# A decoder block on one core: biases in the constant pack, x in four 4 KB-row tiles, half of the transposes behind p's first step

## Chip, cores and metric

The kernel runs on one core of a Trainium2 chip. The metric is device time in microseconds (us), the median of three runs. Before the change it is 675.62 us (675.38 to 676.07).

## What is computed

One residual block on 512 tokens of width 1024. The change touches its front alone: the modulation by `c`, the first normalisation, and the start of the input projection.

```python
c_act = jax.nn.silu(c)
mod = c_act @ ada_w[l] + ada_b[l]
shift1, scale1, gate1, shift2, scale2, gate2 = [m[:, None, :] for m in jnp.split(mod, 6, axis=-1)]
h = rms_norm(x, norm1_g[l]) * (1 + scale1) + shift1
z = h @ w_in[l]
q, k, v, p, g_attn, g_pool = jnp.split(z, split_at, axis=-1)
```

Attention, pooling mixer, gates, output projection and the feed-forward part follow and are the same before and after.

## The kernel before

All is float32. A large product is made of three matmuls: each operand is split into a rounded part (`hi`, on ScalarE, called ACT) and the rest (`lo`, on VectorE, called DVE), and hi.hi, hi.lo and lo.hi are summed in one PSUM bank. There are eight banks of 128 x 512 floats. TensorE is called PE, GpSimd POOL, SyncE SP.

The block's input `h` is wanted transposed: eight tiles `h[k]` of 128 features x 512 tokens. The front makes them so:

- `crow` is silu(c). Two matmuls of a row of ones with it put c on all 128 partitions; ACT copies them to `cbc` (L234).
- x comes as eight tiles of 128 tokens x 512 features, in rows of 2 KB (L164). `rms_rows` sums the squares of a token's two halves, the first on ACT, the second on DVE (L174, L176), adds them on DVE (L180) and takes the power -1/2 on POOL (L182). `scale_x` multiplies each half by it: the first on ACT (L220), the second on DVE (L222), of the last token tile both on ACT (L224).
- PE transposes the scaled x in 32 pieces of 128 x 128 into the eight banks `xT` (L242), token tile by token tile, all before the first matmul of the projection.
- `ada_sum` (L191) makes one modulation value for each of 128 features: DVE multiplies a tile of 128 rows of `ada` by `cbc` and sums along the row. A row holds 1026 floats: 1024 weights, the bias, and a 1 for the two scales (0 elsewhere), and `cbc` ends in two ones, so that the sum is already bias and 1 + scale. There are 48 such tiles, 16 of them (shift and scale for k = 0 to 7) in the front.
- `make_x(k)` copies `xT[k]` out of PSUM with the norm's gain (ACT L248; k = 7 on DVE, L250). `make_h(k)` applies scale and shift on ACT (L280), rounds to `h[k]` hi (L282), and `lo_h` gives the rest on DVE (L287). For k = 0, `gs` (L293) holds gain times scale and `make_h` reads `xT[0]` itself.

The projection's first two products, p (four banks, 128 features each) and q (four banks, 128 tokens each), run k by k: twelve matmuls of p (L135, L138), then twelve of q. Their weights come as tiles p0, q0 (k = 0, 1), p1, q1 and so on, and are split into hi (ACT L109, p0 on DVE L107) and lo (L119: on DVE, q1's on POOL).

PE, ACT and DVE run in the order in which the code is written, each its own; this order is set by hand. The loads are issued by SP in the order of `queue`, and a buffer of the five `wraw` must be free (`pump`): a new load follows a sum or a split. The weights' hi and lo tiles have four buffers each.

Of the kernel before, what the change touches and what calls it, by code (L numbers as in the profile page):

```python
# [51 lines left out]
def block_kernel(tc, x, cvec, ada, wtok, wch, pool_w, wbr, wout, wup, wdn, pack, table, out):  # L52
    nc = tc.nc
# [3 lines left out]
    with ctx:  # L57
        ctx.enter_context(tc.manual_schedule(engines=ENG))
        ep = lambda *a, **k: ctx.enter_context(tc.tile_pool(*a, **k))
        cpool = ep(name="const", bufs=1)  # L60
# [85 lines left out]
        cbc = cpool.tile([P, AW], F32, name="cbc")  # L146
        nc.vector.memset(cbc[:, D:], 1.0)
# [11 lines left out]
        xt = []
        for t in range(TT):  # L160
            row = []
            for f in range(2):
                xi = slot(f"x_{t}_{f}")
                nc.sync.dma_start(xi, x[t * P : (t + 1) * P, f * 512 : (f + 1) * 512])  # L164
                row.append(xi)
            xt.append(row)

        def rms_rows(tiles, name):

            ss = mini.tile([P, 2], F32, tag="ss", name=f"ss_{name}")  # L170
            for f in range(2):
                junk = slot(f"junk_{name}_{f}")
                if f == 0:
                    nc.scalar.activation(junk, tiles[f], AF.Square, scale=1.0 / math.sqrt(D), accum_out=ss[:, f : f + 1])  # L174
# [42 lines left out]
        rss, cbs = [], []  # L217

        def scale_x(t):
            nc.scalar.activation(xt[t][0], xt[t][0], AF.Copy, scale=rss[t])  # L220
            if t < TT - 1:
                nc.vector.tensor_scalar(xt[t][1], xt[t][1], rss[t], None, op0=ALU.mult)  # L222
            else:
                nc.scalar.activation(xt[t][1], xt[t][1], AF.Copy, scale=rss[t])  # L224

        for t in range(TT):
            rs = rms_rows(xt[t], f"x{t}")
            if t < 2:
                cbs.append(bank(f"cb_{t}"))
                nc.tensor.matmul(cbs[t], ones, crow[:, t * 512 : t * 512 + 512], start=True, stop=True)  # L230
            if t:
                scale_x(t - 1)
                if t < 3:
                    nc.scalar.activation(cbc[:, (t - 1) * 512 : t * 512], cbs[t - 1], AF.Copy)  # L234
            rss.append(rs)
        scale_x(TT - 1)

        hh, hl, xs, araw = [], [], {}, {}
        xT = [bank(f"xT_{k}") for k in range(KT)]
        for t in range(TT):  # L240
            for k in range(KT):
                nc.tensor.transpose(  # L242
                    xT[k][:, tslice(t)], xt[t][k // 4][:, (k % 4) * P : (k % 4 + 1) * P], ident)

        def make_x(k):
            xs[k] = slot(f"xs_{k}")
            if k < KT - 1:
                nc.scalar.activation(xs[k], xT[k], AF.Copy, scale=col(C_N1 + k))  # L248
            else:
                nc.vector.tensor_scalar(xs[k], xT[k], col(C_N1 + k), None, op0=ALU.mult)  # L250
# [56 lines left out]
        qps = [bank(f"q_{t}") for t in range(TT)]
        pps = [bank(f"p_{g}") for g in range(TT)]
        for k in range(KT):
            i = k // 2  # L310
# [415 lines left out]
        for t in range(TT):  # L726
            for f in range(2):
                if (t, f) == (0, 0):
                    for t_ in range(2):
                        for f_ in range(2):  # L730
                            out_mm(t_, f_, 0, KT - 2)
                if (t, f) != (3, 0):
                    out_mm(t, f, KT - 2 if t < 2 else 0, KT)
                    out_post(t, f, ops[t, f])
                if late:
                    ada_col(4, late.pop(0))
                    if not late:
# [223 lines left out]
def _layout(a):  # L961
# [32 lines left out]
    arr["pack"] = c(np.concatenate(
        [cols(one("norm1_g")), cols(one("norm2_g")), qk("q_norm_g"), qk("k_norm_g"),
         cols(one("pool_scale")), inv, np.eye(P, dtype=np.float32), cw, cols(one("conv_b"))], axis=1))
# [28 lines left out]
```

## Time and profile before

| | |
|---|---|
| median of three runs | 675.62 us |
| the profiled execution, its time | 675.27 us |
| its span in the profile | 673.3 us |
| PE busy | 662.5 us (98% of the span) |
| DVE, ACT, POOL busy | 518.2, 333.5, 91.8 us |
| HBM read, written | 114.11, 15.75 MB |

The profile is one execution. Its span runs from the first instruction to the last; the time has 2 us more around it. An engine's busy time counts its instructions, not its waits. Names like L191 are lines of the kernel before.

### The profile page before, as it was taken

The page shows a single profiled execution, that of the slowest core. Times are in us where ns is not written, and L with a number is a line of the kernel's source. Part 1 is how long each engine was busy: PE and PEld are TensorE (multiplying, and loading weights), DVE is VectorE, ACT ScalarE, POOL GpSimd, SP SyncE. Part 2 cuts the span into 40 slices and gives each one's busy share as a digit, 9 for nine tenths or more (in the row PEclk, how much of TensorE's full clock was granted, in tenths as well). Part 3 has the DMA queues.
Part 4 walks back from the last instruction along what each step waited for, and adds up shares of the span by engine and source line. Part 5 has one row for each costly group of instructions (what it writes and reads, how often), then busy time and mean ns, then how long its engine had stood idle before and what let it go on. Part 6 is the DMA issues. An engine that isn't in the chain of part 4 may idle for free.

```text
span 673.3 us, 8771 instructions
## 1 busy us (share of the span) xinstructions
PE 662.5 (98%) x3106; PEld 551.4 (82%) x3106; DVE 518.2 (77%) x853; ACT 333.5 (50%) x536; POOL 91.8 (14%) x120
## 2 busy tenths in 40 slices
PE   6999999999999999999999999999999999999997
PEld 4778788888888788888998888888888888888885
DVE  5786876887877688876578878878787878878774
ACT  6545256765564656503653443425344344767431
POOL 2202150000000054603011111120110000001000
PEclk9999999999999999999999999999999999999999
DMA  8795231355543366693257675866835445667741
GB/s 314 274 329 210 93 127 64 109 168 169 176 146 110 94 220 208 193 350 140 80 213 263 212 250 191 307 222 225 298 132 187 165 149 170 213 222 265 250 180 59
DMA packets 41505, 130.43 MB, mean 194 GB/s; under 512 B 5251, under 2 KB 5420, under 8 KB 41462
## 3 DMA queue, kind: packets, MB, share of 16 engines
q1 hardware_dynamic: 35270, 109.82, 47.4%
q0 software_dynamic: 6192, 20.06, 9.0%
q8 instruction: 24, 0.39, 0.2%
q14 instruction: 19, 0.16, 0.1%
HBM read 114.11 MB, written 15.75 MB: 193 GB/s over the span
## 4 chain that ended last, share of the span: by engine, by line
PE 95%; ACT 2%; DVE 1%; issue 1%; DMA 1%; SPq 0%; POOL 0%; DVEq 0%
PE u L129 12%; PE u L128 12%; PE u L130 12%; PE gate_ps L129 4%; PE gate_ps L128 4%; PE gate_ps L130 4%; PE X L892 3%; PE X L890 3%; PE X L891 3%; PE o L128 2%; PE o L130 2%; PE o L129 2%; PE O L495 2%; PE Y L892 1%; PE Y L890 1%; PE Y L891 1%
## 5 line engine op out<-in xcount | busy, mean ns | idle before, releaser
L128 PE MATMUL u<-h2h,hi_up 128*128 128x512 f32 (+1 forms) x384 | 142.7, 372 | 0.0
L129 PE MATMUL u<-h2l,hi_up 128*128 128x512 f32 (+1 forms) x384 | 142.7, 372 | 0.0
L130 PE MATMUL u<-h2h,lo_up 128*128 128x512 f32 (+1 forms) x384 | 142.7, 372 | 0.0
L128 PEld LDWEIGHTS u<-h2h,hi_up 128*128 128x128 f32 x384 | 72.4, 188 | 12.6
L130 PEld LDWEIGHTS u<-h2h,lo_up 128*128 128x128 f32 x384 | 72.4, 188 | 12.5
L129 PEld LDWEIGHTS u<-h2l,hi_up 128*128 128x128 f32 x384 | 72.4, 188 | 12.4
L191 DVE CUSTOM_DVE_ANT_0 raw_ada<-raw_ada,cbc 128x1026 f32<-128x1026 f32 x48 | 60.9, 1293 | 2.9 <-DMA raw_ada<-in_ada 2.6
L760 ACT ACTIVATE uv<-u,pk 128x512 f32<-128x512 f32 x22 | 17.1, 780 | 85.8 <-PE u L130 85.8
L119 DVE TENSOR_TENSOR lo_up<-raw_up,hi_up 128x1024 fp32r<-128x1024 f32 x44 | 52.0, 1219 | 5.8 <-ACT hi_up L109 5.8
L130 PE MATMUL gate_ps<-h_h,lo_gate 128*128 128x512 f32 x128 | 50.0, 390 | 0.0
L129 PE MATMUL gate_ps<-h_l,hi_gate 128*128 128x512 f32 x128 | 49.9, 390 | 0.0
L128 PE MATMUL gate_ps<-h_h,hi_gate 128*128 128x512 f32 x128 | 49.9, 390 | 0.0
L109 ACT ACTIVATE hi_up<-raw_up 128x1024 fp32r<-128x1024 f32 x44 | 44.2, 1048 | 4.3 <-PE u L129 4.3
L813 POOL DMA_DIRECT2D tsum_t<-b x44 | 23.8, 540 | 145.1 <-DVE b L808 138.9
L761 DVE SCALAR_TENSOR_TENSOR uv<-u,pk,uv 128x511 f32<-128x511 f32 x22 | 16.5, 749 | 34.2 <-ACT uv L760 34.2
L119 DVE TENSOR_TENSOR lo_t<-raw_t,hi_t 128x1024 fp32r<-128x1024 f32 (+1 forms) x24 | 26.6, 1129 | 10.4 <-ACT hi_t L109 10.4
L760 ACT ACTIVATE ug<-u,pk 128x512 f32<-128x512 f32 x22 | 17.0, 775 | 32.2 <-PE u L130 32.2
L204 POOL TENSOR_TENSOR wo_l<-raw_wo,wo_h 128x512 fp32r<-128x512 f32 x16 | 25.6, 1619 | 53.6 <-ACT wo_h L203 53.6
L109 ACT ACTIVATE hi_t<-raw_t 128x1024 fp32r<-128x1024 f32 (+1 forms) x24 | 23.7, 987 | 17.9 <-PE Y L892 8.8
L130 PEld LDWEIGHTS gate_ps<-h_h,lo_gate 128*128 128x128 f32 x128 | 24.0, 188 | 5.1
L128 PEld LDWEIGHTS gate_ps<-h_h,hi_gate 128*128 128x128 f32 x128 | 24.0, 188 | 4.6
L129 PEld LDWEIGHTS gate_ps<-h_l,hi_gate 128*128 128x128 f32 x128 | 24.1, 188 | 4.5
(255 smaller groups left out, 1511.3 us busy)
## 6 DMA issues: line engine op xcount, KB each, us to landing
raw_ada<-in_ada SPq DMA_DIRECT2D x48, 513.0 KB, 5.0
raw_up<-in_wup SPq DMA_DIRECT2D x44, 512.0 KB, 4.9
b<-in_wdn SPq DMA_DIRECT2D x44, 256.0 KB, 5.6
tsum_t<-b POOLq DMA_DIRECT2D x44, 256.0 KB, 2.8
raw_t<-tsum_t SPq DMA_DIRECT2D x20, 512.0 KB, 4.5
raw_gate<-in_wch SPq DMA_DIRECT2D x16, 512.0 KB, 5.0
raw_b<-in_wdn SPq DMA_DIRECT2D x15, 512.0 KB, 3.4
raw_br<-in_wbr SPq DMA_DIRECT2D x8, 512.0 KB, 4.5
```

Of the source, the lines that this page charges most:

```text
L109: nc.scalar.activation(hi, raw, AF.Copy)
L119: (nc.gpsimd if nm in pool else nc.vector).tensor_sub(lo, raw, hi.bitcast(F32))
L128: nc.tensor.matmul(ps, sh, mh, start=start, stop=False)
L129: nc.tensor.matmul(ps, sh, ml, start=False, stop=False)
L130: nc.tensor.matmul(ps, sl, mh, start=False, stop=stop)
L191: nc.vector.tensor_tensor_reduce(out=raw, in0=raw, in1=cbc, op0=ALU.mult, op1=ALU.add, scale=1.0, scalar=0.0, accum_out=acol[:, i : i + 1])
L204: (eng or nc.vector).tensor_sub(lo[:, :w], src, hi[:, :w].bitcast(F32))
L760: nc.scalar.activation(t, ps, AF.Identity, scale=cw(2), bias=col(C_CB + i))
L813: nc.gpsimd.dma_start(tsum[n, i][:, u * 512 : u * 512 + 512], b[nm])
L890: nc.tensor.matmul(ps, sh, mh, start=start, stop=False, skip_group_check=True)
L891: nc.tensor.matmul(ps, sh, ml, start=False, stop=False, skip_group_check=True)
L892: nc.tensor.matmul(ps, sl, mh, start=False, stop=stop, skip_group_check=True)
```

## The change

Three things are changed.

1. The biases go to the constant pack (48 columns, `C_AB`), and a row of `ada` has 1024 floats. `ada_sum` starts its sum from the bias (`scalar=`). The 1 of 1 + scale is added by an instruction of its own on DVE for k = 1 to 7, and inside `gs` for k = 0.
2. x comes as four tiles of 128 x 1024, in rows of 4 KB. They lie in two buffers of the hi and two of the lo weights. Each token tile's second half is scaled on DVE, the last one's too.
3. Of the 32 transposes only those of k = 0 to 3 stand ahead of p's k = 0; the other 16 follow it, and q's k = 0 follows them. For k = 0, `h[0]` hi is made on ACT directly from the bank, and the unrounded value on DVE from the bank too. p's k = 0 takes its lo weights before its lo inputs. q1's lo part is made on DVE.

```diff
-                out=raw, in0=raw, in1=cbc, op0=ALU.mult, op1=ALU.add, scale=1.0, scalar=0.0,
+                out=raw, in0=raw, in1=cbc, op0=ALU.mult, op1=ALU.add, scale=1.0, scalar=col(C_AB + i),
...
+        def load_x(t):
+            xi = (whi_p if t < 2 else wlo_p).tile([P, 1024], F32, tag="hi" if t < 2 else "lo", name=f"x_{t}")
+            nc.sync.dma_start(xi, x[t * P : (t + 1) * P])
...
         def sum_h(k):
             for g in range(2):
-                ada_sum(g, k, araw[g, k])
-                held[0] -= 1
-                pump()
+                sum_one(g, k)
+                if g:
+                    nc.vector.tensor_scalar(acols(1, k), acols(1, k), 1.0, None, op0=ALU.add)
...
         def split(name, **kw):
-            ahead(name, 0, pool=("q1",), **kw)
+            ahead(name, 0, **kw)
...
+        scale_x(3, 0, False)
+        flip_x(3, 0)
+        sum_one(0, 0)
+        scale_x(3, 1, True)
+        sum_one(1, 0)
+        gs = mini.tile([P, 1], F32, tag="gs", name="gs")
+        nc.vector.tensor_scalar(gs, acols(1, 0), 1.0, col(C_N1), op0=ALU.add, op1=ALU.mult)
+        make_x(1)
+        his["p0"] = hi_of("p0", early["p0"], True)
...
+        nc.scalar.activation(hh[0], xT[0], AF.Identity, scale=gs, bias=acols(0, 0))
+        split("p0")
+        nc.vector.tensor_scalar(xs[0], xT[0], gs, acols(0, 0), op0=ALU.mult, op1=ALU.add)
         lo_h(0)
...
         sum_h(1)
         split("q0")
         make_h(1)
         lo_h(1)
         sum_h(2)
-        qps = [bank(f"q_{t}") for t in range(TT)]
         pps = [bank(f"p_{g}") for g in range(TT)]
...
+            if k == 0:
+                for k2 in range(4, KT):
+                    xT[k2] = bank(f"xT_{k2}")
+                for t in range(TT):
+                    flip_x(t, 4)
+                for k2 in range(4, KT):
+                    make_x(k2, k2 == 7)
+                qps = [bank(f"q_{t}") for t in range(TT)]
...
-    arr["ada"] = c(np.concatenate(
-        [one("ada_w").T, one("ada_b")[:, None], unit.reshape(6 * D, 1)], axis=1)).reshape(48, P, AW)
+    arr["ada"] = c(one("ada_w").T).reshape(48, P, D)
```

Two places show what the new order does. The first is PE's list around p's and q's k = 0. Before (repeats left out; the brackets name the engines whose signal is awaited), the last transpose, p and q stand in a row, and q's four banks `q_290` to `q_293` wait for ACT alone:

```order
L242 MATMUL xT_190<-pk,x_1_130 128x128
L135 MATMUL p_294<-h_h,hi_p_246 128x512 [waits DVE_49,PE_49,Activation_49]
L135 MATMUL p_297<-h_h,hi_p_246 128x512 [waits DVE_49]
L138 MATMUL p_297<-h_h,lo_p_248 128x512
L135 MATMUL q_290<-hi_q_261,h_h 128x512 [waits Activation_49]
L135 MATMUL q_292<-hi_q_261,h_h 128x512 [waits Activation_49]
L135 MATMUL q_293<-hi_q_261,h_h 128x512 [waits Activation_49]
```

Now p's k = 0 ends, 16 transposes go to the four banks of k = 4 to 7 (`xT_271` to `xT_274`), and q's first four matmuls write the same four banks one after the other:

```order
L138 MATMUL p_258<-h_l,hi_p_214 128x512
L267 MATMUL xT_271<-pk,x_116 128x128 [waits PE_49]
L267 MATMUL xT_274<-pk,x_116 128x128 [waits Activation_49]
L267 MATMUL xT_274<-pk,x_122 128x128
L135 MATMUL q_299<-hi_q_226,h_h 128x512 [waits Activation_49]
L135 MATMUL q_300<-hi_q_226,h_h 128x512 [waits Activation_49]
L135 MATMUL q_301<-hi_q_226,h_h 128x512 [waits Activation_49]
L135 MATMUL q_302<-hi_q_226,h_h 128x512 [waits DVE_49]
L138 MATMUL q_299<-hi_q_226,h_l 128x512
```

What moved: q's k = 0 stood behind p's k = 0 alone; it now stands behind 16 transposes too, and its fourth bank waits for a copy that DVE makes.

The second place is DVE's list from p0's lo part on. Before, the copy of `xT[7]` (`xs_267`) stands ahead of the sums for k = 1 (`raw_ada_231`, `raw_ada_234`) and k = 2 (`raw_ada_237`, `raw_ada_250`):

```order
L119 TENSOR_TENSOR lo_p_248<-raw_p_227,hi_p_246 128x1024 [waits DVE_49]
L287 TENSOR_TENSOR h_l<-xs_241,h_h 128x512 [waits Activation_49]
L250 TENSOR_SCALAR xs_267<-xT_190,pk 128x512 [waits PE_49]
L191 ISA raw_ada_231,acol<-raw_ada_231,cbc 128x1026 [waits DMAHW5_49]
L191 ISA raw_ada_234,acol<-raw_ada_234,cbc 128x1026 [waits DMAHW7_49]
L119 TENSOR_TENSOR lo_q_275<-raw_q_229,hi_q_261 128x1024 [waits DMAHW4_49,Activation_49]
L287 TENSOR_TENSOR h_l<-xs_253,h_h 128x512 [waits Activation_49]
L191 ISA raw_ada_237,acol<-raw_ada_237,cbc 128x1026 [waits DMAHW0_49]
L191 ISA raw_ada_250,acol<-raw_ada_250,cbc 128x1026 [waits DMAHW1_49,DVE_49]
```

Now it stands behind them (`xs_297`, last row), with the additions of 1 (L240) in between:

```order
L119 TENSOR_TENSOR lo_p_220<-raw_p_128,hi_p_214 128x1024 [waits DVE_49]
L306 TENSOR_SCALAR xs_216<-xT_134,gs,acol 128x512 [waits PE_49,Activation_49]
L263 TENSOR_TENSOR h_l<-xs_216,h_h 128x512 [waits DVE_49]
L190 ISA raw_ada_132,acol<-raw_ada_132,cbc,pk 128x1024 [waits DMAHW2_49]
L190 ISA raw_ada_204,acol<-raw_ada_204,cbc,pk 128x1024 [waits DMAHW3_49]
L240 TENSOR_SCALAR acol<-acol 128x1 [waits DVE_49]
L119 TENSOR_TENSOR lo_q_239<-raw_q_130,hi_q_226 128x1024 [waits DMAHW0_49,Activation_49]
L263 TENSOR_TENSOR h_l<-xs_212,h_h 128x512 [waits Activation_49]
L190 ISA raw_ada_208,acol<-raw_ada_208,cbc,pk 128x1024 [waits DMAHW4_49]
L190 ISA raw_ada_222,acol<-raw_ada_222,cbc,pk 128x1024 [waits DMAHW7_49,DMAHW5_49,DVE_49]
L250 TENSOR_SCALAR xs_297<-xT_274,pk 128x512 [waits PE_49]
```

What moved: the copy of the eighth bank went from before the four sums of k = 1 and 2 to behind them, and one copy of the first bank (`xs_216`) came to DVE.

## Rows read from the trace of the kernel before

**Rows 1.** The page: busy time by engine, share of the span, instructions.

```profile
PE 662.5 (98%) x3106; PEld 551.4 (82%) x3106; DVE 518.2 (77%) x853; ACT 333.5 (50%) x536; POOL 91.8 (14%) x120
```

**Rows 2.** Waits of PE, whole span: total us, times, longest.

```profile
PE p L135 <- ACT h_h L282: 1.4, 2, 0.9
```

**Rows 3.** Timeline of PE, front: start us, us, instruction.

```profile
10.17 5.09 PE L242 MATMUL xT<-pk,x 128*128 128x128 f32 x25 [0.43 <-ACT cbc L234]
15.80 1.94 PE L135 MATMUL p<-h_h,hi_p 128*128 128x512 f32 x4 [0.55 <-ACT h_h L282]
...
19.42 1.29 PE L135 MATMUL q<-hi_q,h_h 128*128 128x512 f32 x4
...
22.39 1.07 PE L135 MATMUL p<-h_h,hi_p 128*128 128x512 f32 x4
...
32.36 1.07 PE L138 MATMUL q<-lo_q,h_h 128*128 128x512 f32 x4
34.33 1.19 PE L135 MATMUL p<-h_h,hi_p 128*128 128x512 f32 x4 [0.90 <-ACT h_h L282]
...
56.67 1.07 PE L135 MATMUL p<-h_h,hi_p 128*128 128x512 f32 x4
```

**Rows 4.** Timeline of DVE, front.

```profile
9.68 0.48 DVE L222 TENSOR_SCALAR x<-x,rs_x 128x512 f32<-128x512 f32 x1
10.09 0.69 DVE L176 CUSTOM_DVE_ANT_0 junk_x<-x 128x512 f32<-128x512 f32 x1
...
11.38 1.23 DVE L191 CUSTOM_DVE_ANT_0 raw_ada<-raw_ada,cbc 128x1026 f32<-128x1026 f32 x1
...
13.91 0.16 DVE L293 TENSOR_TENSOR gs<-acol,pk 128x1 f32<-128x1 f32 x1
...
16.45 0.74 DVE L250 TENSOR_SCALAR xs<-xT,pk 128x512 f32<-128x512 f32 x1
17.11 1.22 DVE L191 CUSTOM_DVE_ANT_0 raw_ada<-raw_ada,cbc 128x1026 f32<-128x1026 f32 x1
...
19.40 1.22 DVE L119 TENSOR_TENSOR lo_q<-raw_q,hi_q 128x1024 fp32r<-128x1024 f32 x1
21.56 0.69 DVE L287 TENSOR_TENSOR h_l<-xs,h_h 128x512 fp32r<-128x512 f32 x1 [0.94 <-ACT h_h L282]
...
24.46 0.08 DVE L191 DVE_READ_ACCUMULATOR2_ANT acol<- 128x1 f32 x1
```

**Rows 5.** Timeline of ACT, the making of h for k = 1.

```profile
20.02 0.84 ACT L280 ACTIVATE xs<-xs,acol 128x512 f32<-128x512 f32 x1
```

**Rows 6.** DMA, us to landing: first x tile (issued at 1.14), first modulation tile (4.88).

```profile
x<-in_x SPq DMA_DIRECT2D x1, 256.0 KB, 2.6
...
raw_ada<-in_ada SPq DMA_DIRECT2D x1, 513.0 KB, 6.5
```

**Rows 7.** Front in three stretches: busy us of PE, PEld, DVE, ACT, POOL; PEclk, DMA share, GB/s.

```profile
4.50:5.50 1.00, 1.00 (x3) 0.48 (x2) 0.00 (x0) 0.01 (x1) 0.00 (x0) 1.00 1.06 404
5.75:8.25 2.50, 1.67 (x4) 0.27 (x2) 1.92 (x7) 1.77 (x4) 0.94 (x2) 1.00 0.89 272
10.10:15.20 5.10, 5.03 (x25) 4.85 (x25) 4.90 (x12) 3.43 (x8) 1.20 (x2) 1.00 1.02 414
```

**Rows 8.** Timeline of DVE, two sums from 28 us on.

```profile
28.19 3.42 DVE L191 CUSTOM_DVE_ANT_0 raw_ada<-raw_ada,cbc 128x1026 f32<-128x1026 f32 x1
...
31.54 1.22 DVE L191 CUSTOM_DVE_ANT_0 raw_ada<-raw_ada,cbc 128x1026 f32<-128x1026 f32 x1
```

**Rows 9.** Timeline of POOL, q1's lo part and the four fills.

```profile
28.04 2.49 POOL L119 TENSOR_TENSOR lo_q<-raw_q,hi_q 128x1024 fp32r<-128x1024 f32 x1 [16.19 <-ACT hi_q L109]
30.59 2.03 POOL L400 MEMSET kz<- 64x512 f32 x4
```

**Rows 10.** The front transposes, 10.1 to 14 us: count, ns min/median/max, first and last start.

```profile
L242 PE MATMUL xT<-pk,x x18: 421/421/478, 10.2 to 13.9; 128*128 128x128 f32 x18
```

**Rows 11.** Later transposes of the same size, same columns.

```profile
L688 PE MATMUL hT<-pk,xn x32: 270/272/274, 313.5 to 328.1; 128*128 128x128 f32 x32
```

More of the change, by code (lines that the diff above doesn't have):

```diff
@@ L45 @@
 C_ID = C_INV + 64
-C_EARLY = C_ID + P
+C_AB = C_ID + P
+C_EARLY = C_AB + 48
 C_CW = C_EARLY
@@ L145, in block_kernel @@
         col = lambda i: pk[:, i : i + 1]
-        cbc = cpool.tile([P, AW], F32, name="cbc")
-        nc.vector.memset(cbc[:, D:], 1.0)
+        cbc = cpool.tile([P, D], F32, name="cbc")
         crow = wraw_p.tile([P, 1024], F32, tag="raw", name="crow")[0:1]
@@ L156, in block_kernel @@
         acol = cpool.tile([P, 48], F32, name="acol")
[L159 to L166, printed above, removed]
+        xt, xh = [], []
+        def load_x(t):
+            xi = (whi_p if t < 2 else wlo_p).tile([P, 1024], F32, tag="hi" if t < 2 else "lo", name=f"x_{t}")
+            nc.sync.dma_start(xi, x[t * P : (t + 1) * P])
+            xt.append(xi)
+            xh.append([xi[:, :512], xi[:, 512:]])
         def rms_rows(tiles, name):
+            ms = mini.tile([P, 1], F32, tag="ms", name=f"ms_{name}")
             ss = mini.tile([P, 2], F32, tag="ss", name=f"ss_{name}")
@@ L173, in rms_rows @@
                 if f == 0:
-                    nc.scalar.activation(junk, tiles[f], AF.Square, scale=1.0 / math.sqrt(D), accum_out=ss[:, f : f + 1])
+                    nc.scalar.activation(
+                        junk, tiles[f], AF.Square, scale=1.0 / math.sqrt(D), accum_out=ss[:, f : f + 1])
                 else:
@@ L215, in bias_table @@
                 nc.gpsimd.dma_start(fd[:, c0 : c0 + n], fsb[i][:H, :n])
[L217 to L236, printed above, removed]
-        hh, hl, xs, araw = [], [], {}, {}
[L239 to L250, printed above, removed]
+        hh, hl, xs, araw = [], [], {}, {}
         queue = [(0, 0), (1, 0), "p0", "q0", (0, 1), (1, 1), (0, 2), (1, 2), "p1", "q1", (0, 3), (1, 3),
@@ L287, in lo_h, with flip_x, scale_x @@
             nc.vector.tensor_sub(hl[k], xs[k], hh[k].bitcast(F32))
-        pump()
-        sum_h(0)
+        def flip_x(t, k0):
+            for k in range(k0, k0 + 4):
+                nc.tensor.transpose(xT[k][:, tslice(t)], xt[t][:, k * P : (k + 1) * P], ident)
+        def scale_x(t, f, on_dve):
+            if on_dve:
+                nc.vector.tensor_scalar(xh[t][f], xh[t][f], rss[t], None, op0=ALU.mult)
+            else:
+                nc.scalar.activation(xh[t][f], xh[t][f], AF.Copy, scale=rss[t])
+        for t in range(TT):
+            load_x(t)
+        pump()
+        rss, xT = [], {}
+        for k in range(4):
+            xT[k] = bank(f"xT_{k}")
+        cbs = [bank("cb_0"), bank("cb_1")]
+        for f in range(2):
+            nc.tensor.matmul(cbs[f], ones, crow[:, f * 512 : f * 512 + 512], start=True, stop=True)
+        for t in range(TT):
+            rss.append(rms_rows(xh[t], f"x{t}"))
+            if t:
+                scale_x(t - 1, 0, False)
+                scale_x(t - 1, 1, True)
+                flip_x(t - 1, 0)
+            if t in (1, 2):
+                nc.scalar.activation(cbc[:, (t - 1) * 512 : t * 512], cbs[t - 1], AF.Copy)
+        scale_x(3, 0, False)
[3 more added lines that the diff above has]
+        sum_one(1, 0)
         gs = mini.tile([P, 1], F32, tag="gs", name="gs")
-        nc.vector.tensor_mul(gs, acols(1, 0), col(C_N1))
+        nc.vector.tensor_scalar(gs, acols(1, 0), 1.0, col(C_N1), op0=ALU.add, op1=ALU.mult)
+        make_x(1)
+        his["p0"] = hi_of("p0", early["p0"], True)
         xs[0] = slot("xs_0")
-        make_h(0, xT[0], gs)
-        split("p0", on_dve=True)
+        hh.append(slot("h_0_h", F32R))
+        hl.append(slot("h_0_l", F32R))
+        nc.scalar.activation(hh[0], xT[0], AF.Identity, scale=gs, bias=acols(0, 0))
+        split("p0")
+        nc.vector.tensor_scalar(xs[0], xT[0], gs, acols(0, 0), op0=ALU.mult, op1=ALU.add)
         lo_h(0)
-        for k in range(1, KT):
-            if k == 5:
-                his["q0"] = hi_of("q0", early["q0"])
+        his["q0"] = hi_of("q0", early["q0"])
+        for k in range(2, 4):
             make_x(k)
@@ L314, in block_kernel @@
             cs = [slice(c0 + g * P, c0 + (g + 1) * P) for g in range(TT)]
-            mm3s([(pps[g], pw[0][:, cs[g]], pw[1][:, cs[g]], hh[k], hl[k]) for g in range(TT)], k == 0, k == KT - 1)
+            mm3s([(pps[g], pw[0][:, cs[g]], pw[1][:, cs[g]], hh[k], hl[k]) for g in range(TT)], k == 0, k == KT - 1,
+                 late=k == 0)
+            if k == 0:
+                for k2 in range(4, KT):
+                    xT[k2] = bank(f"xT_{k2}")
+                for t in range(TT):
+                    flip_x(t, 4)
+                for k2 in range(4, KT):
+                    make_x(k2, k2 == 7)
+                qps = [bank(f"q_{t}") for t in range(TT)]
             if k + 2 < KT:
@@ L737, in block_kernel @@
                     if not late:
-                        nc.vector.tensor_mul(acol[:, 32:40], acol[:, 32:40], pk[:, C_N2 : C_N2 + 8])
+                        nc.vector.scalar_tensor_tensor(acol[:, 32:40], acol[:, 32:40], 1.0, pk[:, C_N2 : C_N2 + 8],
+                                                       op0=ALU.add, op1=ALU.mult)
             out_norm(t)
@@ L995, in _layout @@
         [cols(one("norm1_g")), cols(one("norm2_g")), qk("q_norm_g"), qk("k_norm_g"),
[L996 removed]
+         cols(one("pool_scale")), inv, np.eye(P, dtype=np.float32), cols(one("ada_b")), cw, cols(one("conv_b"))], axis=1))
     hot = np.zeros((NB + 1, NF), np.float32)
```

19 lines of the change are left out of this document (12 added, 7 removed).

## The prediction, made before the change was run

> **What bounds the kernel now.** I read the page's busy times first, then PE's waits, then the timelines of the front. PE is busy 98% of the span [rows 1], and almost all that it ever waits for once its matmuls run densely lies in the front: 1.4 us for `h` [rows 2]. The kernel is a front that feeds PE, and behind it a stream that PE alone bounds. So the change is worth what it moves PE's arrival at a point behind the front.
>
> In PE's timeline [rows 3] the reader should see: 25 transposes without a break from 10.17, p's k = 0 at 15.80, q's at 19.42, p's k = 1 at 22.39. From there to the last four of q's k = 2 at 32.36 lie 44 matmuls in 9.97 us, 0.227 us each, 2.72 us a block of twelve. That block ends at 33.27, and p's k = 3 starts at 34.33: 1.06 us idle. From 34.33 to p's k = 7 at 56.67 stand eight blocks, 21.75 us of work in 22.34: 0.59 us more is lost in small pieces. PE has thus 1.65 us of slack between p's k = 1 and p's k = 7, which swallows a late arrival, but no more than that.
>
> **The change part by part, DVE first**, since the new order makes PE wait for it. In DVE's timeline [rows 4] the first two sums start at 11.38 and the next at 13.91 is `gs`; the copy of `xT[7]` stands at 16.45, the sums for k = 1 at 17.11, q0's lo part at 19.40, `h[1]`'s lo part at 21.56 (0.94 us of waiting ahead of it), the end of the sums for k = 2 at 24.54 (24.46 and 0.08).
>
> - Last x tile's second half, scaled on DVE between the first two sums: 9.68 to 10.09, +0.41.
> - The unrounded `h[0]` from the bank, new on DVE: as the bank copy, 16.45 to 17.11, +0.66. The copy of `xT[7]` leaves this place: -0.66. The sums for k = 1 so start at 17.11 + 0.41 = 17.52.
> - Two sums take 2.29 (17.11 to 19.40) and end at 19.81. The 1 of 1 + scale, an instruction of one column like `gs` (0.16, with its start some 0.2), ends at 20.01. `h[1]` follows on ACT in the 1.54 us that it takes now (20.02 to the DVE instruction behind it at 21.56) [rows 5]: 21.55. q0's lo part on DVE lies beside this and is done by 21.2.
> - So DVE is at `h[1]`'s lo part at 21.56 as before; what was added went into its 0.94 us of idle time. The sums for k = 2 end at 24.54, as now.
> - Behind them the second 1 (0.2) and, new in this place, the copy of `xT[7]` (0.74): 25.48.
>
> q's k = 0 now writes the banks of `xT[4]` to `xT[7]`, and its fourth matmul waits for that copy. Behind it in PE's order stands everything. Nine matmuls remain of the block, 2.04 us: p's k = 1 starts at 27.52 in place of 22.39, 5.13 later. PE then has the 1.65 us of slack to give: the waits for `h[3]` and later tiles are gone when PE comes 5 us later to instructions whose inputs come no later. 5.13 - 1.65 = **+3.5 us** at p's k = 7, and behind it PE waits no more.
>
> **x in 4 KB rows** can move DVE's chain earlier as a whole. In the front DVE runs at the pace of the transfers: the first modulation tile, issued at 4.88, lands 6.5 us later [rows 6], at 11.38, just when DVE takes it. While x comes, the DMA rate is 404 GB/s for a time and then 272 for 2.5 us; the modulation's 4 KB rows come at 414 [rows 7]. The same bytes in the slow stretch at 404 would take 1.68 us: a gain of 0.8. The lower bound is 0, since 404 was reached in 2 KB rows too. The upper bound is DVE's own: the first tile lands 2.6 us after its issue at 1.14 [rows 6], at 3.7, and DVE needs 1.29 us for each of four token tiles (10.09 to 11.38), so it can't be at the first sum before 8.9, 2.5 earlier. I take 0.8, the row that stands nearest, because the slow stretch lies wholly in x's transfer. The Trainium skill (DMA: Bandwidth & Descriptors, Specifications) has rows of 512 B and more at line rate; by it 2 KB rows lose nothing, the gain is 0 and the sum is +3.5. The 404 agrees with it, the 272 doesn't.
>
> **PE's own path** is shorter and hidden. `gs` at 14.32, `h[0]` hi on ACT 0.84: p's k = 0 starts at about 15.3 in place of 15.80. It takes 2.72 and up to 0.9 of waiting as now, the 16 moved transposes at most 0.2 each (25 in 5.09 [rows 3]), 3.3: done by 22.2, three bank copies on ACT by 24.3. DVE's copy ends at 25.48 and covers this. If the cover went (DVE 1.2 us earlier with PE not), PE's path would be the wait.
>
> **Parts that cost nothing.** Two columns less in a sum are two thousandths of it. The biases add 48 columns, 25 KB, to the constant load; at 414 GB/s [rows 7] that is 0.06 us, ahead of the first transposes only. q1's lo part on DVE costs 1.2 us there, but DVE's sum beside POOL's took 3.42 in place of 1.22 [rows 8] while POOL worked on that part [rows 9]; both lie behind the point above, where PE is the later one. x's tiles hold two hi and two lo buffers till the transposes end, some 22; the next weights' hi parts (p1's) want them at 26. The whole tile must land before ACT's first square; DVE's half waited for the second half anyway. On SP four issues go, and the loads of p0, q0 no longer wait for x tiles; the order of the bytes is the same.
>
> **The sum.** 3.5 - 0.8 = +2.7 us. The profiled execution took 675.27, so 677.97; it lies 0.35 under the median of the three runs, so against that the number is **678.3**.
>
> **The rivals.**
>
> 1. *The rows' length does nothing* (0.15). DVE's chain starts at 11.38 as now: 675.6 + 3.5 = 679.1. For it the 404 in 2 KB rows, against it the 272.
> 2. *The clock* (0.05). The front's transposes take 421 ns [rows 10], those behind 313 us 272 [rows 11], though the PEclk column says 1.00 in the front too [rows 7]: by the durations PE was at its lower level, 1.2 GHz, until it had transposed without a break from 10.17 on. Now its 16 early transposes come in four groups with gaps, so p's k = 0 may start low. At half rate all of it is 5.44, and the transposes behind 3.2: PE's path ends at 15.3 + 8.6 + 2 = 26.0 and not 25.5, so 678.8. The Trainium skill (TensorE: Matmul & The Clock Gate, The HAM clock gate) says that idling is the slow state and steady matmuls end it; the 421 and 272 agree.
> 3. *POOL's fills* (0.05). Without q1's lo part, POOL does its four fills, 2.03 us, at about 12, beside DVE's first sums. The sum at 31.54 beside the fills took its 1.22, so I price it at 0. The Trainium skill (GPSIMD Engine Reference, Key points) has POOL share its SBUF interfaces with DVE and names contention for two-input instructions; if the fills hold the sums up as the lo part did, DVE loses up to 2.0: 680.3. The 3.42 agrees with it, the 1.22 doesn't.
> 4. *The front runs early enough* (0.17): not slower. x keeps up with DVE and its chain starts 2.5 earlier: 3.5 - 2.5 = +1.0, 676.6, no change that can be told. It decides at 2.1: the copy of `xT[7]` must end before 23.4. For it that SP issues p0 and the modulation tiles without waiting; against it that x's last three tiles would have to come at 400 GB/s and more without one slow stretch (1.57 MB between 3.7 and 7.6). 0.12 of it stays within the bound; 0.05 is left for a chain still earlier, which would be faster.
>
> **How the numbers follow.** The forecast with its 0.8 has 0.58, the rivals 0.15, 0.05, 0.05 and 0.17. 0.2% is 1.35 us, about what a measurement of this kernel can tell from no change: 674.3 to 677.0. Slower: 0.58 + 0.25 = 0.83; same 0.12; faster 0.05. The range reaches from rival 4 (676.6) to rivals 1 and 2 together (679.6), with 0.3 at either end, by which single runs of the kernel differ: 676.3 to 679.9. Left out are rival 3 and what is faster still.
>
> **What would show it.** Right: in PE's timeline a gap of over 1 us inside q's k = 0, between its third and fourth matmul, ended by DVE's copy (L250 in the new file); no wait at p's k = 3; the first sum on DVE at about 10.6. Wrong: q's k = 0 done before 25; PE waiting elsewhere for `h` or weights; a first sum at 9 (rival 4) or 11.4 (rival 1); sums longer than 1.3 us beside fills (rival 3); the wait ended by ACT's copies (rival 2).

## The result, and the profile after

The changed kernel takes **680.89 us** (median of 4 runs, 679.37 to 682.57), the kernel before beside it 675.50 (4 runs, 675.31 to 676.07): a ratio of 1.0079, 95% interval 1.0055 to 1.0104. It is slower, as forecast, but by 5.4 us and not by 2.7, and it lies outside the range. The profiled execution took 679.37, the shortest of the four, so two gaps are to be explained: 4.1 us in that execution where the sum had 2.7, and a median 1.5 us above that execution.

The page after, busy time by engine, and two of PE's waits (total us, times, longest):

```profile
PE 663.9 (98%) x3106; PEld 551.8 (81%) x3106; DVE 521.9 (77%) x862; ACT 332.5 (49%) x534; POOL 89.6 (13%) x119
```

```profile
PE p L135 <- ACT h_h L304: 1.7, 1, 1.7
PE q L135 <- DVE xs L250: 1.3, 1, 1.3
```

The second wait is new: PE waits for DVE's copy of `xT[7]`. The wait for `h` at p's k = 3 [rows 2, 3] is gone; the one for `h` that is left (1.7) stands ahead of p's k = 0. PE's timeline after:

```profile
14.82 2.07 PE L135 MATMUL p<-h_h,hi_p 128*128 128x512 f32 x4 [1.71 <-ACT h_h L304]
16.69 1.91 PE L138 MATMUL p<-h_h,lo_p 128*128 128x512 f32 x4
18.40 1.91 PE L138 MATMUL p<-h_l,hi_p 128*128 128x512 f32 x4
20.10 1.97 PE L267 MATMUL xT<-pk,x 128*128 128x128 f32 x16
22.52 1.65 PE L135 MATMUL q<-hi_q,h_h 128*128 128x512 f32 x3 [0.45 <-ACT xs L252]
25.47 0.50 PE L135 MATMUL q<-hi_q,h_h 128*128 128x512 f32 x1 [1.29 <-DVE xs L250]
...
27.66 1.07 PE L135 MATMUL p<-h_h,hi_p 128*128 128x512 f32 x4
...
33.11 1.07 PE L135 MATMUL p<-h_h,hi_p 128*128 128x512 f32 x4
...
60.31 1.07 PE L135 MATMUL p<-h_h,hi_p 128*128 128x512 f32 x4
```

The gap inside q's k = 0 stands where it was forecast, between the third and the fourth matmul, ended by DVE's copy. p's k = 1 comes at 27.66 in place of 22.39 (+5.27) and p's k = 7 at 60.31 in place of 56.67 [rows 3] (+3.64): 1.63 of slack was given back, where 1.65 was read. From 16.69 to 18.40 four matmuls take 1.71, so p's k = 0 ran at PE's lower level.

DVE's timeline after, and the front in the second stretch of [rows 7] (last three columns: PEclk, DMA share, GB/s):

```profile
10.22 0.16 DVE L179 TENSOR_TENSOR ms_x<-ss_x 128x1 f32<-128x1 f32 x1 [0.54 <-ACT junk_x L173]
...
10.69 1.28 DVE L190 CUSTOM_DVE_ANT_0 raw_ada<-raw_ada,cbc,pk 128x1024 f32<-128x1024 f32 x1
...
11.89 0.61 DVE L271 TENSOR_SCALAR x<-x,rs_x 128x512 f32<-128x512 f32 x1
12.43 1.27 DVE L190 CUSTOM_DVE_ANT_0 raw_ada<-raw_ada,cbc,pk 128x1024 f32<-128x1024 f32 x1
...
15.73 0.81 DVE L306 TENSOR_SCALAR xs<-xT,gs,acol 128x512 f32<-128x512 f32 x1
16.57 0.69 DVE L263 TENSOR_TENSOR h_l<-xs,h_h 128x512 fp32r<-128x512 f32 x1
17.18 1.28 DVE L190 CUSTOM_DVE_ANT_0 raw_ada<-raw_ada,cbc,pk 128x1024 f32<-128x1024 f32 x1
...
21.47 0.69 DVE L263 TENSOR_TENSOR h_l<-xs,h_h 128x512 fp32r<-128x512 f32 x1 [0.46 <-ACT h_h L258]
...
24.68 0.74 DVE L250 TENSOR_SCALAR xs<-xT,pk 128x512 f32<-128x512 f32 x1
```

```profile
5.75:8.25 2.50, 2.07 (x6) 0.71 (x4) 1.94 (x6) 2.20 (x5) 0.89 (x2) 1.00 1.03 408
```

The slow stretch of x's transfer is gone: 408 GB/s in place of 272 [rows 7], and the first sum starts at 10.69 in place of 11.38 [rows 4]. Ahead of it DVE now waits for ACT (0.54, ACT's square of the last x tile) and no longer for a transfer. The copy of `xT[7]` starts at 24.68, where the prediction's chain less its 0.8 had 23.94: DVE lost 0.74 on the way.

### The profile page after: what moved, and what is told of

The parts are those of the page before. It is cut to its first block, busy times and chain, and to the rows that moved or that the text cites. A ratio compares the mean times of both kernels' runs of the same rounds, so it can differ in the third digit from the quotient of the medians.

```text
span 677.3 us, 8766 instructions
## 1 busy us (share of the span) xinstructions
PE 663.9 (98%) x3106; PEld 551.8 (81%) x3106; DVE 521.9 (77%) x862; ACT 332.5 (49%) x534; POOL 89.6 (13%) x119
## 4 chain that ended last, share of the span: by engine, by line
PE 95%; DVE 2%; ACT 1%; DMA 1%; issue 0%; SPq 0%; ACTq 0%
PE u L129 12%; PE u L128 12%; PE u L130 12%; PE gate_ps L130 4%; PE gate_ps L129 4%; PE gate_ps L128 4%; PE X L908 3%; PE X L910 3%; PE X L909 3%; PE q L138 2%; PE o L128 2%; PE o L130 2%; PE o L129 2%; PE p L138 2%; PE O L512 2%; PE Y L908 1%
## 5 line engine op out<-in xcount | busy, mean ns | idle before, releaser
L190 DVE CUSTOM_DVE_ANT_0 raw_ada<-raw_ada,cbc,pk 128x1024 f32<-128x1024 f32 x48 | 61.2, 1300 | 1.9 <-DMA raw_ada<-in_ada 1.9
```

The costliest lines, as they stand in the source:

```text
L190: nc.vector.tensor_tensor_reduce(out=raw, in0=raw, in1=cbc, op0=ALU.mult, op1=ALU.add, scale=1.0, scalar=col(C_AB + i), accum_out=acol[:, ...
```

## Experiments

Ten kernels were run, each timed beside the kernel before on the same chip, whose median there lay between 675.5 and 675.7.

**again** is the changed kernel a second time, and **warm** adds 17 transposes of the identity into a spare bank, so that PE works from the first transposes of x on:

```diff
+        def fill_pe(n):
+            for i in range(n):
+                nc.tensor.transpose(warm[:, tslice(i % 4)], ident, ident)
...
                 flip_x(t - 1, 0)
+                fill_pe(3)
...
         flip_x(3, 0)
+        fill_pe(8)
```

> The changed kernel once more, for more executions and a second trace. Its times lie 679.4 to 682.6 us where the kernel before keeps within 0.8. Theory A (the clock): TensorE starts p's k = 0 at the lower level, and when it reaches the higher one differs from execution to execution; the slow executions have a longer low stretch, seen as matmuls of p's or q's k = 0 at double length and as a lower mean granted clock. Then the times spread over 3 us again, and the trace's end goes with the point where the clock rises. Theory B (the transfers): x or the modulation tiles land at other times. Then the clock is the same in all traces and DVE's first sum moves. Rival: the spread was chance, and all executions are at 679.4.

> The changed kernel with 17 more transposes of the identity, into a spare bank, between the early transposes and ahead of p's k = 0, so that TensorE has few gaps there. They add nothing to the result. Theory A (the clock): p's k = 0 then runs at the higher level (2.7 to 3.6 us in place of 5.3), the executions lie within 1 us of each other, and the median is near 679.4, since q's fourth matmul still waits for DVE's copy at 25.4. Theory B (the transfers): the spread of 3 us stays. Rival: the clock costs nothing and the extra transposes delay the early ones: 680 or more.

Measured: again 680.95 (5 runs, 679.71 to 682.35), ratio 1.0079 [1.0066, 1.0092]; warm 681.45 (4 runs, 681.19 to 681.78), 1.0086 [1.0072, 1.0100]. The profiled execution of again was its longest, 682.35, and it shows what the first profile doesn't. Its PE timeline:

```profile
22.25 1.65 PE L135 MATMUL q<-hi_q,h_h 128*128 128x512 f32 x3 [1.01 <-ACT xs L252]
25.66 0.79 PE L135 MATMUL q<-hi_q,h_h 128*128 128x512 f32 x1 [1.76 <-DVE xs L250]
26.25 1.91 PE L138 MATMUL q<-hi_q,h_l 128*128 128x512 f32 x4
27.96 1.91 PE L138 MATMUL q<-lo_q,h_h 128*128 128x512 f32 x4
29.67 1.91 PE L135 MATMUL p<-h_h,hi_p 128*128 128x512 f32 x4
31.37 1.30 PE L138 MATMUL p<-h_l,hi_p 128*128 128x512 f32 x4
...
63.37 1.07 PE L135 MATMUL p<-h_h,hi_p 128*128 128x512 f32 x4
```

And two stretches of the change's profile, of again and of warm (busy us of PE, PEld, DVE, ACT, POOL; PEclk, DMA share, GB/s):

```profile
22.00:25.00 3.00, 1.56 (x4) 0.56 (x3) 2.96 (x7) 1.83 (x4) 0.00 (x0) 1.00 0.87 322
25.00:31.80 6.80, 6.33 (x28) 5.23 (x29) 5.66 (x7) 3.14 (x4) 0.00 (x0) 1.00 0.78 254
```

```profile
22.00:25.00 3.00, 1.50 (x3) 0.56 (x3) 2.96 (x7) 1.37 (x4) 0.00 (x0) 1.00 0.88 311
25.00:31.80 6.80, 6.14 (x14) 4.78 (x15) 5.66 (x7) 3.33 (x4) 0.00 (x0) 0.50 0.74 237
```

```profile
22.00:25.00 3.00, 1.80 (x3) 0.66 (x3) 2.96 (x7) 1.37 (x4) 0.00 (x0) 0.70 0.84 294
25.00:31.80 6.80, 6.26 (x18) 4.99 (x19) 5.66 (x7) 3.20 (x4) 0.00 (x0) 0.63 0.81 275
```

Behind the waits in q's k = 0 the granted clock is 0.50, PE's lower level, from 25 to 31.8 us in again, 0.63 of full speed on average in warm, and 1.00 in the change's profile. 28 matmuls fit into that stretch in the change's profile and 14 in again's. q's fourth matmul comes only 0.19 later in again than in the change's profile (25.66 and 25.47), DVE's copy with it, but p's k = 7 comes 3.06 later (63.37 and 60.31), and the execution is 2.98 longer. So it isn't the first rise of the clock that costs, as I had thought when I made warm (in warm p's k = 0 did run at the full level, and the kernel took 681.45 where I expected 679.4): the clock **falls again** in some executions. The mean granted clock that each run carries goes with it in the change: 0.999 in its runs of 679.4 and 679.7, 0.995 to 0.997 in those of 680.8 to 682.6. By itself that mean proves nothing: a run of x4k (below) has 0.997 and is no slower than the rest (675.16).

**x7_early** moves the sums for k = 2 behind the copies of `xT[4]` to `xT[7]`, so that DVE's copy comes first.

```diff
-        sum_h(2)
         pps = [bank(f"p_{g}") for g in range(TT)]
...
                     make_x(k2, k2 == 7)
                 qps = [bank(f"q_{t}") for t in range(TT)]
+                sum_h(2)
```

> The changed kernel with the sums for k = 2 moved behind the copy of xT[7] on DVE. If that copy is what q's k = 0 waits for, it ends at 22.8 in place of 25.4, q's k = 0 is paced by ACT's three copies (to 23.7), and the kernel is 1.3 us faster than the changed one, execution for execution (678.1 where that has 679.4). Rival, TensorE's own path (p's k = 0 at the low clock, then 16 transposes): no gain.

Measured: 677.64 (9 runs, 677.07 to 677.99), ratio 1.0028 [1.0018, 1.0038]. PE's timeline:

```profile
22.52 1.66 PE L135 MATMUL q<-hi_q,h_h 128*128 128x512 f32 x4 [0.56 <-ACT xs L252]
...
25.86 1.07 PE L135 MATMUL p<-h_h,hi_p 128*128 128x512 f32 x4
...
58.49 1.07 PE L135 MATMUL p<-h_h,hi_p 128*128 128x512 f32 x4
```

The gap of 1.29 is gone, p's k = 1 and p's k = 7 both come 1.8 earlier than in the change (1.3 was expected), and all runs lie within 0.9: 3.3 us below the change's median, 1.8 by the copy and 1.5 by a clock that stays up (0.999 or 1.000 in all nine runs). q's k = 0 still stands behind the transposes here, 2.1 us above the kernel before.

**q_late** leaves every engine's order but PE's: q's k = 0 goes behind p's k = 1.

```diff
-            mm3s([(qps[t], hh[k][:, tslice(t)], hl[k][:, tslice(t)], qw[0][:, ws], qw[1][:, ws])
-                  for t in range(TT)], k == 0, k == KT - 1, late=1)
+            for kq in ((0, 1) if k == 1 else (k,) if k else ()):
+                wq = slice(kq % 2 * 512, kq % 2 * 512 + 512)
+                mm3s([(qps[t], hh[kq][:, tslice(t)], hl[kq][:, tslice(t)], qw[0][:, wq], qw[1][:, wq])
+                      for t in range(TT)], kq == 0, kq == KT - 1, late=1)
```

> The change with q's k = 0 moved behind p's k = 1 on PE, so that p's k = 1 doesn't stand behind DVE's copy of xT[7]; DVE, ACT and the transfers keep their order. My theory (the copy of xT[7] is what q's k = 0, and all behind it, waits for; the moved transposes themselves cost PE their 2 us): p's k = 1 starts right behind the transposes once h[1]'s lo part is there, at 22.1 to 22.4, q's k = 0 follows at 24.9 without a wait, p's k = 2 at 30.4 in place of 27.83 before, 2.5 later; 1.65 of it goes into the slack up to p's k = 7: 0.9 us above the kernel before, 676.5. Rival (PE's own work, 16 more transposes and the low clock of p's k = 0, is the cost, whatever it waits for): p's k = 2 no earlier than 32 and 679 or more.

Measured: 676.62 (11 runs, 676.43 to 676.81), ratio 1.0015 [1.0006, 1.0023].

```profile
21.46 1.20 PE L135 MATMUL p<-h_h,hi_p 128*128 128x512 f32 x4 [0.41 <-ACT h_h L258]
...
25.44 0.50 PE L135 MATMUL q<-hi_q,h_h 128*128 128x512 f32 x1 [0.28 <-DVE xs L250]
...
30.38 1.07 PE L135 MATMUL p<-h_h,hi_p 128*128 128x512 f32 x4
```

p's k = 2 comes at 30.38, to a tenth where expected, in part by luck: p's k = 1 starts 0.6 earlier than I had it, and q's fourth matmul still waits 0.28 for DVE's copy, where I expected no wait. The copy is as late as ever, but p's k = 1 stands ahead of it. Of the change's 5.4 us 4.3 are thus the place of q's k = 0 in PE's list, the 1.5 of the clock among them. About 1 is left for the rest of the change together; no run takes apart what of it the transposes in PE's stream cost.

**gapfill** keeps the wait and fills it: `zz` is a tile of zeros.

```diff
+        def keep(n):
+            for i in range(n):
+                nc.tensor.matmul(pps[i % TT], zz, hh[0], start=False, stop=False)
...
+            for n, (ps, sh, sl, mh, ml) in enumerate(ops):
+                if before:
+                    keep(before[n])
...
-                  for t in range(TT)], k == 0, k == KT - 1, late=1)
+                  for t in range(TT)], k == 0, k == KT - 1, late=1, before=(2, 2, 2, 6) if k == 0 else ())
```

> The change with twelve matmuls of a zero tile added to q's k = 0 (two ahead of each of its first three matmuls, six ahead of the fourth), which add 0 to p's banks while PE would wait for the copies of xT[4] to xT[7]. Nothing else waits less: q's fourth matmul still comes behind DVE's copy at about 25.4 us. Theory A' (the changed kernel's median lies 1.5 us above its profiled execution because the granted clock falls again while PE waits inside q's k = 0): the clock doesn't fall between 22 and 32 us, every execution lies within 0.6 us, at 679.2 to 680.0. Rival (the executions above 680 come from something else, such as late transfers): the executions spread from 679.4 to 682.4 as before and the median stays at 680.9. If PE's zero matmuls themselves hold q up, p's k = 1 starts later than 27.7 by up to 0.4.

Measured: 679.44 (5 runs, 678.95 to 679.71), ratio 1.0055 [1.0043, 1.0068].

```profile
24.84 1.53 PE L324 MATMUL p<-h_h,zz 128*128 128x512 f32 x6
26.21 0.39 PE L137 MATMUL q<-hi_q,h_h 128*128 128x512 f32 x1
...
28.25 1.07 PE L137 MATMUL p<-h_h,hi_p 128*128 128x512 f32 x4
```

```profile
25.00:31.80 6.80, 6.80 (x31) 5.62 (x31) 5.65 (x7) 3.35 (x4) 0.00 (x0) 1.00 0.76 269
```

The zero matmuls hold q's fourth up by 0.7 and p's k = 1 by 0.6 (I had allowed 0.4), and yet the median is 1.5 below the change's, with a granted clock of 1.00 in this stretch and no execution above 679.71; the five lie within 0.8. That decides it: what lies between 679.4 and 680.9 is the clock that falls when PE waits in q's k = 0. Here work kept it up that adds nothing to the result.

**x4k** and **pack** are the kernel before with one part of the change each: x in four tiles of 4 KB rows, and biases in the constant pack (in pack the data's layout as in the change).

```diff
+            xi = (whi_p if t < 2 else wlo_p).tile([P, 1024], F32, tag="hi" if t < 2 else "lo", name=f"x_{t}")
+            nc.sync.dma_start(xi, x[t * P : (t + 1) * P])
+            xt.append([xi[:, :512], xi[:, 512:]])
...
```

```diff
...
-                out=raw, in0=raw, in1=cbc, op0=ALU.mult, op1=ALU.add, scale=1.0, scalar=0.0,
+                out=raw, in0=raw, in1=cbc, op0=ALU.mult, op1=ALU.add, scale=1.0, scalar=col(C_AB + i),
...
+                if g and k:
+                    nc.vector.tensor_scalar(acols(1, k), acols(1, k), 1.0, None, op0=ALU.add)
...
```

> The kernel before with x in four tiles of 4 KB rows, and nothing else of the change. In the changed kernel's trace DVE's first sum starts at 10.69 in place of 11.38. Theory: the rows did that, and here all of the front comes 0.7 us earlier: 674.8 in place of 675.5. Rival 1: the gain came from the new order; then 675.5. Rival 2: something behind (the stall of DVE's sum beside POOL, the loads of p1 and q1) takes it back: 675.5, with DVE's first sum early all the same.

Measured: 675.23 (11 runs, 675.02 to 675.66), ratio 0.9994 [0.9985, 1.0003]: not to be told from the kernel before, as rival 2 had it.

```profile
5.75:8.25 2.50, 2.08 (x6) 0.79 (x5) 1.88 (x6) 2.18 (x5) 1.12 (x2) 1.00 1.02 416
```

```profile
10.71 1.22 DVE L188 CUSTOM_DVE_ANT_0 raw_ada<-raw_ada,cbc 128x1026 f32<-128x1026 f32 x1
...
12.49 1.23 DVE L188 CUSTOM_DVE_ANT_0 raw_ada<-raw_ada,cbc 128x1026 f32<-128x1026 f32 x1 [0.55 <-DMA raw_ada<-in_ada]
...
27.89 3.42 DVE L188 CUSTOM_DVE_ANT_0 raw_ada<-raw_ada,cbc 128x1026 f32<-128x1026 f32 x1
```

```profile
34.04 1.21 PE L135 MATMUL p<-h_h,hi_p 128*128 128x512 f32 x4 [0.88 <-ACT h_h L279]
```

DVE's first sum comes 0.67 earlier, but the second modulation tile isn't there yet and takes 0.55 back. p's k = 3 comes 0.29 earlier than before [rows 3], still behind a wait of 0.88 for `h[3]`. In the change there is no such wait: DVE scales half an x tile in that place (11.89), and the transfers are faster. From 8.5 to 11.5, x4k and then the change:

```profile
8.50:11.50 3.00, 2.57 (x13) 2.17 (x12) 2.42 (x7) 2.58 (x7) 1.45 (x2) 1.00 0.59 237
```

```profile
8.50:11.50 3.00, 1.81 (x8) 1.36 (x8) 2.45 (x7) 2.58 (x6) 1.71 (x3) 1.00 1.02 419
```

x4k_q1dve, direct_h0 and combo, which also have x in 4 KB rows beside modulation rows of 1026 floats, have 231 to 249 GB/s in that stretch; the kernel before has 418 and pack 421. Why the transfers slow down in these four isn't shown. x4k also has four loads of x in place of eight, so that SP issues the first modulation tile at 2.96 in place of 4.88; no run takes the length of the rows and the number of loads apart.

> The kernel before with part 1 alone: biases in the constant pack, 1024-float rows, the 1 added by an instruction of its own. The prediction's price for it is nothing that reaches the end. From the trace of the change: each sum 0.05 longer (1.20 in place of 1.15 from start to start), the added 1 about 0.1 with its start: over the eight sums and three added 1s up to h[3] that makes 0.6 to 0.8 on DVE's chain, and the wait at p's k = 3 (0.90) grows by that. Behind it stand 0.59 us of small waits up to p's k = 7 that can give some back: 675.8 to 676.3. If the sums' length is hidden: 675.5.

Measured: 676.49 (11 runs, 675.92 to 677.40), ratio 1.0014 [1.0005, 1.0023], a little above what I expected.

```profile
11.93 1.28 DVE L190 CUSTOM_DVE_ANT_0 raw_ada<-raw_ada,cbc,pk 128x1024 f32<-128x1024 f32 x1
...
29.20 3.41 DVE L190 CUSTOM_DVE_ANT_0 raw_ada<-raw_ada,cbc,pk 128x1024 f32<-128x1024 f32 x1
...
33.86 0.15 DVE L271 TENSOR_SCALAR acol<-acol 128x1 f32<-128x1 f32 x1
```

```profile
35.58 1.21 PE L135 MATMUL p<-h_h,hi_p 128*128 128x512 f32 x4 [1.43 <-ACT h_h L283]
```

A sum takes 1.28 in place of 1.22, and the added 1 stands between the last sum and `h[3]`: the wait at p's k = 3 is 1.43 in place of 0.90. In this execution DVE's first sum is late by 0.55 too (11.93); whether that belongs to the part or to the one execution stays open, and so how much of the 1.0 us the sums' form and the added 1 cost.

**x4k_q1dve** is x4k with q1's lo part on DVE, **direct_h0** adds `h[0]` hi made by ACT from the bank (with it the copy of `xT[7]` goes to ACT, and p's k = 0 takes its lo weights first), and **combo** adds p1's hi and lo parts ahead of `h[2]`; the main lines of the three edits one after the other:

```diff
-            ahead(name, 0, pool=("q1",), **kw)
+            ahead(name, 0, **kw)
```

```diff
-        make_h(0, xT[0], gs)
-        split("p0", on_dve=True)
...
+        nc.scalar.activation(hh[0], xT[0], AF.Identity, scale=gs, bias=acols(0, 0))
+        split("p0")
+        nc.vector.tensor_scalar(xs[0], xT[0], gs, acols(0, 0), op0=ALU.mult, op1=ALU.add)
```

```diff
+                if k == 0:
+                    his["p1"] = hi_of("p1", early["p1"])
                 make_h(k + 2)
+                if k == 0:
+                    split("p1")
...
```

> The kernel before with x in 4 KB rows (as in x4k) and q1's lo part on DVE in place of POOL. In x4k DVE's sum beside POOL's lo part still takes 3.4 us and PE waits 0.88 at p's k = 3 for h[3]. Theory (that sum is what sets h[3]): the lo part costs DVE 1.15 and gives back 2.2, h[3] comes 1 us earlier and the wait of 0.88 goes: 674.3 to 674.6, faster than the kernel before. Rival (the small waits behind p's k = 3 only grow by what is saved, since ACT and the loads for k = 4 set them): 675.0 to 675.3, as x4k.

> x4k_q1dve with one more piece of part 3 and no transpose moved: h[0] hi on ACT directly from the bank, the unrounded h[0] on DVE from the bank, p's k = 0 with its lo weights first; the copy of xT[7] goes to ACT so that DVE's list stays as long. PE's first matmul of p comes 0.6 earlier, at 14.75. Theory (what counts is PE's arrival behind p's k = 3, and h[3], which DVE's sums and lo parts set, isn't earlier): the 0.6 come back as a wait of 0.4 to 0.6 at p's k = 3, where now there is none; 674.0 to 674.4, the same as x4k_q1dve. Rival (an earlier p's k = 0 is worth what it is earlier): 673.7.

> direct_h0 with p1's hi part on ACT ahead of h[2], in its 3 us of idle time, and p1's lo part on DVE ahead of h[2]'s lo part, in its 1.5 us of idle time, so that the sums for k = 3 come 1.2 us earlier. Theory: h[3] comes 1.2 earlier, PE waits nowhere between p's k = 0 and k = 7, and the 0.4 to 0.6 of the earlier start reach the end: 673.6 to 673.9. Rival (p1's weights land only at 24 us or later, and hold up h[2] on ACT): a wait at p's k = 2 and 674.5 or more.

Measured: x4k_q1dve 674.29 (11 runs, 674.07 to 675.24), ratio **0.9985** [0.9976, 0.9993]: faster than the kernel before, by a margin whose interval leaves out 1 but which is under the 0.2% named ahead, and so faster than the change too. DVE's first sum for k = 3 takes 1.22 again and not 3.42, and p's k = 3 has no wait any more:

```profile
28.90 1.22 DVE L188 CUSTOM_DVE_ANT_0 raw_ada<-raw_ada,cbc 128x1026 f32<-128x1026 f32 x1
```

```profile
32.85 1.21 PE L135 MATMUL p<-h_h,hi_p 128*128 128x512 f32 x4
```

direct_h0 took 675.13 (11 runs, 673.97 to 676.77), 0.9991 [0.9982, 1.0000], combo 673.89 (9 runs, 673.59 to 676.84), 0.9985 [0.9974, 0.9997]. direct_h0's median missed the 674.0 to 674.4 expected; combo's lies in its range, but its ratio, which counts all runs, is no better than x4k_q1dve's. Both missed what I expected of p's k = 0, as direct_h0's row shows:

```profile
16.61 1.19 PE L135 MATMUL p<-h_h,hi_p 128*128 128x512 f32 x4 [2.90 <-DVE xs L297]
```

PE waits for DVE's new copy (L297), which reads the bank of `xT[0]` until 16.57, so p's first bank is presumably that one: PE starts 1.24 later than in x4k_q1dve (15.37), not 0.6 earlier. Its profiled execution still took 674.12, but not by the theory, which had a difference come back as a wait at p's k = 3, where neither execution waits: 0.91 of the 1.24 is gone by q's k = 0 already, since p's k = 0 takes 2.87 there (16.61 to 19.48) and 3.78 in x4k_q1dve (15.37 to 19.15), whose first four matmuls of p take 1.94. The runs of both fall into two groups, direct_h0's five from 673.97 to 674.24 at a mean clock of 0.998 or 0.999, and six from 675.13 up at 0.995 to 0.997; x4k_q1dve's three longest (675.10 to 675.24) have 0.997 too. That has the look of the change's second fall, but no slower execution of these was profiled, so it isn't shown.

## Why the prediction was right and wrong

- **The mechanism of the wait was right**: q's k = 0 behind the transposes, its fourth bank waiting for DVE's copy, p's k = 1 five us late, 1.63 of slack given back, no wait behind it. x7_early, which takes that wait away, comes down to 677.64, and q_late, which leaves 0.28 of it, to 676.62.
- **x in 4 KB rows**: +0.8 was taken, 0.69 measured (11.38 to 10.69). The rate rose as named (408 and 416 GB/s where 272 stood), but the transfers no longer set the start of the first sum: its modulation tile, issued at 2.96, lands 7.2 us later, at 10.2, and DVE comes to it only at 10.69, held up by ACT's square of the last x tile. That the size came out near is thus in part luck. Rivals 1 (nothing) and 4 (2.5) both fall. Rival 4 took 1.29 us of DVE for a token tile, and the last one took 1.70 (from 8.99, the start of its sum of squares, to 10.69). The Trainium skill (DMA: Bandwidth & Descriptors, Specifications), by which 2 KB rows would lose nothing, doesn't fit the 272 and, in pack, 269 GB/s, though the number of loads differs as well.
- **DVE's chain was mis-sized by 0.74.** "Two columns less in a sum are two thousandths of it" failed: the form with the bias as a column takes 1.28 and not 1.22, start to start 1.20 and not 1.15, which makes 0.2 over the four sums for k = 1 and 2 (the first two took no longer than before, 2.51 without x's half, 2.53 before). The bank copy with two columns cost 0.84 up to its follower and not 0.66, x's half 0.54 and not 0.41, `gs` and the first 1 about 0.1 more; the first sum was 0.1 later than taken. That makes 0.7 of the 0.74. I priced new forms by the rows of old ones, and in this chain, which ends in a wait of PE's, each excess counted in full. pack, which has the sums' form, the new `gs` and the added 1 without the rest, was 1.0 us slower, but part of that may be its late first sum.
- **Behind the copy**: 2.24 from its end to p's k = 1, not 2.04. And the end of the span lies 3.2 us behind the last operation's end in the execution after (673.42 + 0.69 to 677.3), 2.9 in the one before (669.71 + 0.69 to 673.3) and 3.2 in x4k (669.47 + 0.69 to 673.4), so about 0.3 of the 4.1 looks like a trait of that one execution before and not the change's. With 0.74 and 0.20 that is 1.24 of the 1.4 missing; the rest isn't traced.
- **The step that failed is the price of the wait, and the clock put the result outside the range.** With the clock up, as in the executions of 679.4 and 679.7, it would lie within. Rival 2 had PE start low in p's k = 0 and gave that 0.5. It did start low (5.28 from p's first matmul to the transposes where 2.72 was taken), but cost nothing by that: the 16 transposes took 1.97 where 3.3 was taken, and DVE's copy, at 25.42, still ended after all of PE's own path. What neither the sum nor a rival had is that a wait of over a us, put into a stretch that had none, can make the clock fall *again*, and that in again all of p's and q's matmuls up to 31 us then take 0.43 in place of 0.227. I priced the wait at its length, within the 5.13 by which p's k = 1 is late; it cost its length and in most executions 1.5 to 3.2 us more. The Trainium skill (TensorE: Matmul & The Clock Gate, The HAM clock gate) says that the idle state is the slow one and that the place of a change of level differs between runs of one kernel. again against the change's profile agrees: the last four matmuls of p's k = 0 start at 18.40 in both and take 1.09 in the one and 1.91 in the other, and the later fall is in the one alone.
- **A reading of before**: the 0.9 us that p's k = 0 took there above 2.72 I read as waiting. By the durations most of it is PE's lower level: its first four matmuls take 1.78 from start to start (15.80 to 17.58), and four at the lower level 1.71.
- **POOL's fills** (rival 3): the sums beside them took the same 1.27 and 1.28 as those behind, so the rival falls. POOL's timeline after has them at 11.24:

```profile
11.24 2.19 POOL L417 MEMSET kz<- 64x512 f32 x4
```

  The scaling of x's half at 11.89 took 0.61 beside them, 0.48 without (at 10.29 in the same execution, and [rows 4]). The Trainium skill (SBUF — State Buffer, Who interferes with whom) has a copy or scaling that uses both of DVE's ports contend with POOL, and a sum of two inputs only with POOL work that reads; the rows agree with that for the sums, as do the 3.42 beside q1's lo part and its absence in x4k_q1dve; whether the scaling uses both ports no row says.

## What to carry to other kernels

A wait that is moved into a dense stream of matmuls is not priced by its length alone: ask whether PE's clock can fall in it, and if the wait can't be reordered away (as in q_late), filling it with idle work bounded the loss here (gapfill, 679.44 against 680.89). Where a chain on one engine ends in such a wait, price each new form of an instruction (a column for a constant, a bank for a buffer) as a range, since all excesses add up. Look at the times and the granted clock of every run and not of the profiled one alone, and profile a slower execution before a cause is named: here the profile that was read first was the one execution in four that didn't show the largest cost.

## What the runs showed of the hardware that was not expected

The granted clock fell from 1.00 to 0.50 within a kernel that keeps PE 98% busy, with PE's two waits in q's k = 0 (1.01 and 1.76 us in again) ahead of it; in the change's profile, with 0.45 and 1.29 there, it stayed at 1.00. With zero matmuls in the gap no execution of five shows the fall, by its time and its mean clock. DVE's multiply-and-sum takes 1.28 us with a column as its start value and 1.22 with a constant, with two columns fewer to read. And the PEclk column says 1.00 at the front of each profile even where four matmuls of 512 columns take 1.71 us (16.69 to 18.40) against 0.91 at full speed: there the durations decide, not the column.
